# Layer 1's norm statistics from 16 products, with gate projections and VectorE/GpSimd work reordered in layer 0

## The chip, the cores and the metric

The kernel runs on one core of one Trainium2 chip. The core has a matrix engine (TensorE, PE in the profile, with its weight loads as PEld), VectorE (DVE), ScalarE (ACT), GpSimd (POOL) and SyncE (SP), whose queue issues the DMAs. The metric is the device time of one execution in microseconds (us), as a median over runs.

## The reference, cut to what matters

A two-layer trunk over x of 512 tokens x 1024 channels, in float32. Each layer computes `x + rmsnorm(mixer(rmsnorm(x)))`.

```python
# layer 0: 16 SSD heads in 4 groups, 16 forgetting-attention heads, one projection in and one out
proj = einsum('bsd,de->bse', rmsnorm(x), w_in)        # z_ssd, z_fox, x/B/C, dt, q, k, v, f
xbc = silu(causal_depthwise_conv(xbc, conv_w, conv_b))   # width 4
y = ssd_chunked(xs, dt, a, bm, cm) + xs * d_skip      # chunks of 128; decay matrices exp(segment sums)
y = group_rmsnorm(y * silu(z_ssd))
o = forgetting_attention(q, k, v, log_f) * silu(z_fox)
out = einsum('bse,ed->bsd', concatenate([y, o]), w_out)
# layer 1
val, glu_gate, z = split(einsum('bsd,de->bse', rmsnorm(x), w_in))
h = causal_depthwise_conv(val * sigmoid(glu_gate), conv_w, conv_b)   # 2048 channels, width 31
h = silu(layernorm(h, ln_g, ln_b)) * silu(z)          # mean and variance over the 2048 channels
out = einsum('bse,ed->bsd', h, w_out)
```

## The kernel before, in words

**Products in three parts.** Every float32 operand of a large product is split into a high part (`hlh`, `uh`, `w`: a cast on ACT) and a low part (`hll`, `ul`: source minus high part, on DVE or POOL); each product is then three products of PE in a reduced float32 (`mm3`, L109).

**Jobs.** The input projection of layer 0 is a list of 48 jobs, numbered from 0, each of 24 products of 512 columns (or 48 of 256) with 512 KB of weights. SP loads a job's weights into one of two raw buffers `wr` (`wload`); `wsplit` casts them on ACT to `w` (L155, L157) and subtracts the low part on the job's engine `j.eng` (L119). Without other word `j.eng` is DVE for even and POOL for odd jobs (`Job`). Before the change the jobs are: B, C and two x tiles of group 0; eight `z_ssd`; B, C, x, x of groups 1, 2 and 3; four gate projections `z_fox(0..3)`; then `v_proj`, `qk_proj` for the eight pairs of heads, with `z_fox(4..7)` two after pair 1 and two after pair 2. A job's last action evacuates its PSUM bank: a width-4 convolution on ACT and DVE for B, C and x (`cv`), an ACT copy for the gates (`zf`), splits for q, k and v. For layer 1 most low parts are computed ahead during layer 0 (`lo_ahead`: `pre` loaded, `prh` cast on ACT, subtracted on DVE, stored as `lo`), so that layer 1 only casts.

**Steps between the products.** PE's order is written by hand (`manual_schedule` for PE); the other engines' queues are filled in an order that a scheduler picks, in which the weight casts have priority. `Steps` deals out the SSD and attention work between chunks of the projection's products: each step has needs with delays, counted in estimated PE time (`now`), and the remaining steps are spread evenly over the remaining chunks. SSD, per group g: Silu of B, C, x (`silus`), low parts of B and C on POOL, tokens-major transposes (`xt`, `Bt`), `cb`, and for each of four heads `seg` (segment sums, four DVE instructions, then Exp on ACT), `mprod` (L1331: `seg` times `cb` on DVE, then cast to `hlh` on ACT and low part `hll` on POOL) and `ydiag` (12 products of 64 columns into `yd`), then states, gate and norm. Attention, per head: four `sa` (scores `s`, negated maximum on DVE, Exp `pr` on ACT, scaling on POOL), four `sb` (transposes `pT`, split `ph`, `pl`), one `sc` (`o`). `fox_silus(a)` is the Silu of four gates in place (`zf<-zf`); it runs once its four projections are there. Silu and Exp need different tables on ACT: a switch is an ACT_TABLE_LOAD.

**From layer 0 to layer 1.** After the output projection, `done0` norms each block of 128 tokens into `u`; `to_uT` (L362) transposes `u` on PE into `uT` banks, from which ACT makes `uh1` (L375, in PSUM reads of 256 tokens) and DVE `ul1` (L380). It is called for layer 0 at the very start, and for layer 1 twice, for the first and the second half of the tokens. The first four jobs of layer 1 (small weight tiles `ws`) run on the first half and then on the second. A weight cast looks at the list `evacs`: it is queued behind the last listed ACT instruction that was issued at least three jobs earlier (`cast`, L151). Only the Sigmoid and z evacuations of layer 1 entered themselves there (`evacuated`).

**Layer 1.** Sixteen tiles of 128 channels: value and gate products, GLU, then 31 convolution taps shared by DVE (`lane`), ACT with POOL (`pool_stream`, `prod` and `acc`) and, for the last two tiles, PE. `tile_end` squares the finished tile `cvo` on ACT to `sq`, and keeps running totals `Ssum` and `Qsum` on POOL, of the first 14 tiles. `stats1` then sums over channels: for each of four token blocks and both totals, three one-column products (total, tile 14, tile 15) into one bank `st`; DVE and POOL make mean and `rstd`, and `stats2` spreads them over partitions by products (`mu`, `rs`). Two z jobs stand on PE between `stats1` and `stats2`, one behind it; then the output projection starts with `lnorm` (DVE), Silu and split per tile.

Of the kernel before, what the change touches and what calls it, by code (L numbers as in the profile page):

```python
# [11 lines left out]
AF = mybir.ActivationFunctionType  # L12
ALU = mybir.AluOpType
# [5 lines left out]
NB = S // P  # L19
# [17 lines left out]
def trunk(  # L37
# [7 lines left out]
    V, G, A, T = nc.vector, nc.gpsimd, nc.scalar, nc.tensor  # L45
# [55 lines left out]
    def mm(o, l, r, start, stop):  # L101
        T.matmul(o, l, r, start=start, stop=stop, skip_group_check=True)  # L102
        now[0] += max(o.shape[-1] / 2400 + 0.014, 0.11)
# [10 lines left out]
    def tok(b):  # L114
        return slice(b * P, (b + 1) * P)
# [5 lines left out]
    def hilo(src, n=S, eng=None, s="hl", cast=None):  # L121
        h, l = t2(s + "h", F32R)[:, :n], t2(s + "l", F32R)[:, :n]
        split(h, l, src, cast or A.copy, eng or V)
        return h, l
# [23 lines left out]
    def evacuated(i):  # L148
        evacs.append((state["run"], i.ins))
# [71 lines left out]
    jobs = []  # L221
# [140 lines left out]
    def to_uT(uh, ul, half, us, g0):  # L362
        for kp in range(KT // 2):
            pb = bank("uT")
            for j in range(2):
                k = 2 * kp + j
                for b in range(2):
                    tr(pb[:, j * 256 + b * P : j * 256 + (b + 1) * P],
                                us[b][k // 4][:, k % 4 * P : (k % 4 + 1) * P], ident)
            for j in range(2):  # L370
                k = 2 * kp + j
                sl = slice(half * 256, half * 256 + 256)
                src = pb[:, j * 256 : (j + 1) * 256]
                g = g0[:, k : k + 1]
                A.activation(uh[k][:, sl], src, AF.Copy, scale=g)  # L375
            for j in range(2):
                k = 2 * kp + j
                src = pb[:, j * 256 : (j + 1) * 256]
                g = g0[:, k : k + 1]
                V.scalar_tensor_tensor(ul[k][:, sl], src, g, f32(uh[k])[:, sl], ALU.mult, ALU.subtract)  # L380
# [39 lines left out]
    pb = bank("pv")  # L420
# [89 lines left out]
    def xbc(kind, i):  # L510
        base, t0 = BASE[kind]

        def evac(pb):
            bcx[kind, i] = conv4(pb, t0 + i)
            done[kind, i] = now[0]
        return fm_job(e_w_in, base + i * P, evac, uh, ul)
# [51 lines left out]
    def z_fox(j):  # L568
        def evac(pb):
            oT[j] = t2("zf")  # L570
            A.copy(oT[j], pb)
            done["zf", j] = now[0]
        fm_job(e_w_in, C_ZF + j * P, evac, uh, ul)
# [130 lines left out]
    z_ssd(0)  # L704
    z_ssd(1)
    for g in range(1, 4):
        xbc("B", g)
        xbc("C", g)
        xbc("x", 2 * g)
        xbc("x", 2 * g + 1)  # L710
    for j in range(4):
        z_fox(j)
    for j in range(8):
        if j % 2 == 0:
            v_proj(j // 2)
        qk_proj(j)
        if j in (1, 2):
            for i in range(2):
                z_fox(2 + 2 * j + i)

    x1, us1 = [], []
    uh1, ul1 = {}, {}
# [247 lines left out]
    def tile_end(j, a):  # L970
        o = acc[j]
        if not NPT[j // 2]:
            A.copy(o, a)
        sq = t2("sq")
        A.activation(sq, o, AF.Square)
        sums.append((o, sq))
        if len(sums) == 2:
            n = [t2("Ssum"), t2("Qsum")]
            for i in range(2):
                G.tensor_tensor(n[i], sums[0][i], sums[1][i], ALU.add)  # L980
            tot.extend(n)
        elif 2 < len(sums) <= NT - 2:
            for i in range(2):
                G.tensor_tensor(tot[i], tot[i], sums[-1][i], ALU.add)

    tot = []
    lanes = [lane(0), lane(1)]
# [42 lines left out]
    def stats1():  # L1030

        pb = bank("st")
        parts = [tot, sums[-2], sums[-1]]
        for b in range(NB):
            for i in range(2):
                o = pb[:, 4 * i + b : 4 * i + b + 1]
                for n, t in enumerate(parts):
                    mm(o, t[i][:, tok(b)], ones[:, 0:1], n == 0, n == 2)
        mq = st["mq"] = col("mq", 8)
        V.tensor_scalar(mq, pb[:, :8], 1.0 / 2048, None, ALU.mult)  # L1040
        va = col("va", 4)
        V.tensor_tensor(va, mq[:, :4], mq[:, :4], ALU.mult)
        V.tensor_tensor(va, mq[:, 4:8], va, ALU.subtract)
        V.tensor_scalar(va, va, 0.0, EPS, ALU.max, ALU.add)
        rs = st["r"] = col("rstd4", 4)
        G.tensor_tensor(rs, va, mhalf.to_broadcast([P, 4]), ALU.pow)
        for i, c in enumerate((mq, rs)):
            dm = st["d", i] = t2("dm")
            for b in range(NB):
                V.tensor_scalar(dm[:, tok(b)], ident, c[:, b : b + 1], None, ALU.mult)  # L1050
# [278 lines left out]
    def mprod(h):  # L1329
        s = ms[h]  # L1330
        V.tensor_tensor(s, s, SG[h // 4]["cb"], ALU.mult)  # L1331
        ms[h] = hilo(s, eng=G)

    def ydiag(h):
        st = SG[h // 4]
# [82 lines left out]
    def attention(steps):  # L1418
# [50 lines left out]
        for h in range(16):  # L1469
# [14 lines left out]
                add(("sb", h, i), lambda h=h, i=i: sb(h, i), *need)  # L1484
            add(("sc", h), lambda h=h: sc(h), (("sb", h, 3), 6), (("v", h // 4), 5), (("fs", h // 8), 3))

    early = lo_ahead([j for j in jobs[J1:] if not j.make][:48])
    run(1)
    steps = Steps()
# [78 lines left out]
```

## Time and profile before

| what | value |
|---|---|
| median of 3 timed runs | 984.03 us (981.89 to 984.90) |
| the profiled execution: its time, its span | 978.23 us, 976.5 us |
| mean granted TensorE clock in it | 0.97 |
| PE, DVE, ACT, POOL busy, share of the span | 96%, 74%, 61%, 50% |
| layer 0 with its output projection | 0 to 605 us |
| layer 1's statistics products | 850.8 to 858.0 us |

The page gives busy time by engine, the granted clock of TensorE, the chain of work that ended last, and groups of instructions by line and operation. Timelines list instructions in order of time: start, duration, engine, line, operation, output <- inputs, count, and in brackets how long the engine stood idle before and for whom. Matmuls are pipelined: one row's duration is its latency, and what a product costs is the distance to the next start. A clock of 0.50 means that TensorE runs at half speed.

### The profile page before, as it was taken

The page shows a single profiled execution, that of the slowest core. Times are in us where ns is not written, and L with a number is a line of the kernel's source. Part 1 is how long each engine was busy: PE and PEld are TensorE (multiplying, and loading weights), DVE is VectorE, ACT ScalarE, POOL GpSimd, SP SyncE. Part 2 cuts the span into 40 slices and gives each one's busy share as a digit, 9 for nine tenths or more (in the row PEclk, how much of TensorE's full clock was granted, in tenths as well). Part 3 has the DMA queues.
Part 4 walks back from the last instruction along what each step waited for, and adds up shares of the span by engine and source line. Part 5 has one row for each costly group of instructions (what it writes and reads, how often), then busy time and mean ns, then how long its engine had stood idle before and what let it go on. Part 6 is the DMA issues. An engine that isn't in the chain of part 4 may idle for free.

```text
span 976.5 us, 13762 instructions
## 1 busy us (share of the span) xinstructions
PE 934.1 (96%) x4723; PEld 777.3 (80%) x4723; DVE 718.0 (74%) x1217; ACT 598.3 (61%) x1075; POOL 488.2 (50%) x424
## 2 busy tenths in 40 slices
PE   5999999989999989989999998999999999999996
PEld 5976887777988868878678888888888887787885
DVE  5767868978476758887866246999998989549812
ACT  5556666567456756757674446788696768437500
POOL 2313545243233413533562101999999998439610
PEclk9999999979699999999899998999999999989999
DMA  6636432364446576573527795254664753513422
GB/s 181 209 93 205 151 93 64 104 192 145 138 130 196 170 240 201 181 230 132 187 88 236 257 361 201 81 188 143 218 191 135 233 188 132 163 57 108 141 75 108
DMA packets 180266, 159.84 MB, mean 164 GB/s; under 512 B 7708, under 2 KB 151716, under 8 KB 180196
## 3 DMA queue, kind: packets, MB, share of 16 engines
q1 hardware_dynamic: 180180, 158.96, 50.7%
q8 instruction: 37, 0.61, 0.2%
q14 instruction: 33, 0.27, 0.1%
q10 hardware_dynamic: 16, 0.00, 0.0%
HBM read 129.45 MB, written 29.36 MB: 163 GB/s over the span
## 4 chain that ended last, share of the span: by engine, by line
PE 64%; DVE 11%; issue 7%; DMA 6%; ACT 6%; POOL 5%; SPq 1%; DVEq 0%; ACTq 0%; POOLq 0%
PE m L102 38%; PE o L102 10%; PE tm L102 6%; POOL w L119 3%; PE yd L102 3%; DMA wr<-in_o_w_in_dram 2%; DMA wr<-in_e_w_out_dram 2%; ACT w L157 2%; PE s L102 1%; DVE pre L205 1%; PE acc L102 1%; PE pT L106 1%; ACT pr L95 1%; PE st L102 1%; DVE nmx L1432 1%
## 5 line engine op out<-in xcount | busy, mean ns | idle before, releaser
L102 PE MATMUL m<-uh,w 128*128 128x512 f32 (+1 forms) x1392 | 457.6, 395 | 3.1 <-DVE cv L505 1.9
L102 PEld LDWEIGHTS m<-uh,w 128*128 128x128 f32 x1392 | 262.8, 191 | 55.1 <-issue 3.1
L102 PE MATMUL m<-ul,w 128*128 128x512 f32 (+1 forms) x696 | 268.9, 386 | 0.0
L119 POOL TENSOR_TENSOR w<-wr,w 128x1024 fp32r<-128x1024 f32 x44 | 112.0, 2545 | 164.7 <-ACT w L157 115.6
L961 DVE SCALAR_TENSOR_TENSOR acc<-h,cw,acc 128x490 f32<-128x490 f32 (+14 forms) x272 | 177.6, 728 | 5.2 <-ACT acc L953 4.5
L102 PE MATMUL o<-w,hlh 128*128 128x512 f32 x512 | 161.7, 397 | 2.0 <-ACT pr L95 1.9
L868 POOL TENSOR_TENSOR acc<-acc,prod 128x505 f32<-128x505 f32 (+12 forms) x122 | 156.6, 1285 | 7.4
L102 PEld LDWEIGHTS m<-ul,w 128*128 128x128 f32 x696 | 132.9, 191 | 21.1 <-issue 0.5
L157 ACT CAST w<-wr 128x1024 fp32r<-128x1024 f32 x76 | 79.6, 1049 | 54.2 <-DMA wr<-in_e_w_out_dram 17.3
L102 PEld LDWEIGHTS o<-w,hlh 128*128 128x128 f32 x512 | 94.9, 190 | 21.1 <-ACT pr L95 2.5
L102 PE MATMUL o<-w,hll 128*128 128x512 f32 x256 | 101.2, 395 | 1.8 <-DVE hll L119 1.6
L1438 POOL TENSOR_SCALAR pr<-pr,ri 128x128 f32<-128x128 f32 (+1 forms) x64 | 38.8, 608 | 117.3 <-DVE ri L1437 93.4
L205 DVE TENSOR_TENSOR pre<-pre,prh 128x1024 fp32r<-128x1024 f32 x48 | 71.3, 1486 | 34.5 <-ACT prh L204 34.2
L102 PE MATMUL tm<-w,uh 128*128 128x256 f32 (+1 forms) x384 | 94.8, 339 | 0.6 <-ACT pr L95 0.6
L119 DVE TENSOR_TENSOR w<-wr,w 128x1024 fp32r<-128x1024 f32 x44 | 59.4, 1350 | 35.1 <-ACT w L157 28.0
L854 ACT ACTIVATE prod<-h,cw 128x505 f32<-128x505 f32 (+12 forms) x122 | 77.5, 707 | 0.0
L155 ACT CAST w<-wr 128x1024 fp32r<-128x1024 f32 x56 | 57.6, 1047 | 31.0 <-DMA wr<-in_o_w_out_dram 13.3
L102 PEld LDWEIGHTS tm<-w,uh 128*128 128x128 f32 x384 | 66.1, 200 | 6.5 <-issue 1.1
L341 POOL TENSOR_TENSOR rstd<-var,mhalf 128x1 f32<-128x1 f32 (+1 forms) x20 | 12.9, 644 | 114.2 <-DVE var L339 114.1
L204 ACT CAST prh<-pre 128x1024 fp32r<-128x1024 f32 x48 | 50.5, 1052 | 21.6 <-DVE pre L205 14.0
L102 PE MATMUL tm<-w,ul 128*128 128x256 f32 (+1 forms) x192 | 63.2, 329 | 0.0
L95 ACT ACTIVATE pr<-s,nmx 128x128 f32<-128x128 f32 (+1 forms) x64 | 33.9, 530 | 46.5 <-DVE nmx L1432 32.4
(265 smaller groups left out, 1605.2 us busy)
## 6 DMA issues: line engine op xcount, KB each, us to landing
wr<-in_e_w_in_dram SPq DMA_DIRECT2D x56, 512.0 KB
pre<-in_o_w_in_dram SPq DMA_DIRECT2D x48, 512.0 KB
lo<-pre SPq DMA_DIRECT2D x48, 512.0 KB
wr<-in_o_w_in_dram SPq DMA_DIRECT2D x48, 512.0 KB
w<-lo SPq DMA_DIRECT2D x44, 512.0 KB
wr<-in_e_w_out_dram SPq DMA_DIRECT2D x16, 512.0 KB
wr<-in_o_w_out_dram SPq DMA_DIRECT2D x16, 512.0 KB
x<-in_x_dram SPq DMA_DIRECT2D x12, 256.0 KB
```

What stands on the lines that cost most here:

```text
L95: i = A.activation(*a, **kw)
L102: T.matmul(o, l, r, start=start, stop=stop, skip_group_check=True)
L119: lo_eng.tensor_tensor(lo, src, f32(hi), ALU.subtract)
L155: last_cast[0] = A.copy(hi, src).ins
L157: last_cast[0] = A.copy(hi, src).ins
L204: A.copy(h, t)
L205: V.tensor_tensor(t.bitcast(F32R), t, f32(h), ALU.subtract)
L341: mark["rstd"] = G.tensor_tensor(r, v, mhalf.to_broadcast([P, ss.shape[-1]]), ALU.pow).ins
L854: A.activation(prs[i][:, s:], hs[j][:, : S - s], AF.Copy, scale=w31(30 - s, j))
L868: G.tensor_tensor(a2[j][:, s:], a2[j][:, s:], prs.pop(i)[:, s:], ALU.add)
L961: V.scalar_tensor_tensor(a[:, s:], h[:, : S - s], w31(30 - s, j), a[:, s:], ALU.mult, ALU.add)
L1438: G.tensor_scalar(p[:, :L], p[:, :L], ri, 1.0, ALU.mult, ALU.mult)
```

## The change

Five edits:

- The totals take in tiles 14 and 15, these two adds on DVE, and `stats1` makes 16 products in place of 48.
- `to_uT` for layer 1 enters its ACT reads in `evacs`.
- `z_fox(4..7)` stands ahead of the B, C and x jobs of group 3.
- The low part in `mprod` goes from POOL to DVE.
- The jobs 6 to 39 all subtract on POOL.

```diff
--- before.py
+++ after.py
@@ -372,7 +372,9 @@
                 sl = slice(half * 256, half * 256 + 256)
                 src = pb[:, j * 256 : (j + 1) * 256]
                 g = g0[:, k : k + 1]
-                A.activation(uh[k][:, sl], src, AF.Copy, scale=g)
+                i = A.activation(uh[k][:, sl], src, AF.Copy, scale=g)
+                if state["run"]:
+                    evacuated(i)
             for j in range(2):
                 k = 2 * kp + j
                 src = pb[:, j * 256 : (j + 1) * 256]
@@ -704,6 +706,9 @@
     z_ssd(0)
     z_ssd(1)
     for g in range(1, 4):
+        if g == 3:
+            for j in range(4, 8):
+                z_fox(j)
         xbc("B", g)
         xbc("C", g)
         xbc("x", 2 * g)
@@ -714,9 +719,6 @@
         if j % 2 == 0:
             v_proj(j // 2)
         qk_proj(j)
-        if j in (1, 2):
-            for i in range(2):
-                z_fox(2 + 2 * j + i)
 
     x1, us1 = [], []
     uh1, ul1 = {}, {}
@@ -979,9 +981,9 @@
             for i in range(2):
                 G.tensor_tensor(n[i], sums[0][i], sums[1][i], ALU.add)
             tot.extend(n)
-        elif 2 < len(sums) <= NT - 2:
+        elif len(sums) > 2:
             for i in range(2):
-                G.tensor_tensor(tot[i], tot[i], sums[-1][i], ALU.add)
+                (G if len(sums) <= NT - 2 else V).tensor_tensor(tot[i], tot[i], sums[-1][i], ALU.add)
 
     tot = []
     lanes = [lane(0), lane(1)]
@@ -1030,12 +1032,9 @@
     def stats1():
 
         pb = bank("st")
-        parts = [tot, sums[-2], sums[-1]]
-        for b in range(NB):
-            for i in range(2):
-                o = pb[:, 4 * i + b : 4 * i + b + 1]
-                for n, t in enumerate(parts):
-                    mm(o, t[i][:, tok(b)], ones[:, 0:1], n == 0, n == 2)
+        for i in range(2):
+            for b in range(NB):
+                mm(pb[:, 4 * i + b : 4 * i + b + 1], tot[i][:, tok(b)], ones[:, 0:1], True, True)
         mq = st["mq"] = col("mq", 8)
         V.tensor_scalar(mq, pb[:, :8], 1.0 / 2048, None, ALU.mult)
         va = col("va", 4)
@@ -1329,7 +1328,7 @@
     def mprod(h):
         s = ms[h]
         V.tensor_tensor(s, s, SG[h // 4]["cb"], ALU.mult)
-        ms[h] = hilo(s, eng=G)
+        ms[h] = hilo(s)
 
     def ydiag(h):
         st = SG[h // 4]
@@ -1484,6 +1483,8 @@
                 add(("sb", h, i), lambda h=h, i=i: sb(h, i), *need)
             add(("sc", h), lambda h=h: sc(h), (("sb", h, 3), 6), (("v", h // 4), 5), (("fs", h // 8), 3))
 
+    for j in jobs[6:40]:
+        j.eng = G
     early = lo_ahead([j for j in jobs[J1:] if not j.make][:48])
     run(1)
     steps = Steps()
```

ACT's queue where layer 1's input is transposed (`uh` here is `uh1`, `junk` a sum of squares of the next token block, `wr` the raw weights). Before:

```order
L375 ACTIVATE uh_1333_6103<-uT_6119,c_130 128x256
L375 ACTIVATE uh_1335_6105<-uT_6119,c_130 128x256
L157 CAST w_6569<-wr_6567 128x1024
L375 ACTIVATE uh_1337_6107<-uT_6128,c_130 128x256
L375 ACTIVATE uh_1339_6109<-uT_6128,c_130 128x256
L375 ACTIVATE uh_1341_6111<-uT_6137,c_130 128x256
L375 ACTIVATE uh_1343_6113<-uT_6137,c_130 128x256
L157 CAST w_6574<-wr_6572 128x1024
L375 ACTIVATE uh_1345_6115<-uT_6146,c_130 128x256
L375 ACTIVATE uh_1347_6117<-uT_6146,c_130 128x256
L348 ACTIVATE junk_6165,ss_6164<-o_1252_5746 128x512
```

After the change:

```order
L375 ACTIVATE uh_1333_6103<-uT_6119,c_130 128x256
L375 ACTIVATE uh_1335_6105<-uT_6119,c_130 128x256
L375 ACTIVATE uh_1337_6107<-uT_6128,c_130 128x256
L375 ACTIVATE uh_1339_6109<-uT_6128,c_130 128x256
L375 ACTIVATE uh_1341_6111<-uT_6137,c_130 128x256
L375 ACTIVATE uh_1343_6113<-uT_6137,c_130 128x256
L375 ACTIVATE uh_1345_6115<-uT_6146,c_130 128x256
L375 ACTIVATE uh_1347_6117<-uT_6146,c_130 128x256
L348 ACTIVATE junk_6165,ss_6164<-o_1252_5746 128x512
L348 ACTIVATE junk_6183,s_1362_6182<-o_1244_5731 128x512
```

The two casts between the `uh` reads have gone; they, and the two casts that stood ahead of this piece, now come later, between the products of layer 1's first two tiles.

ACT's queue where the second four gates get their Silu. Before, inside attention (`pr` is the Exp of scores `s`):

```order
L95 ACTIVATE pr_3640,rs_3641<-s_3634,nmx_3638 128x128
L571 COPY zf_3646<-m_3537 128x512
L95 ACT_TABLE_LOAD
L95 ACTIVATE zf_2985<-zf_2985 128x512
L95 ACTIVATE zf_3067<-zf_3067 128x512
L95 ACTIVATE zf_3535<-zf_3535 128x512
L95 ACTIVATE zf_3646<-zf_3646 128x512
L95 ACT_TABLE_LOAD
L95 ACTIVATE pr_3677,rs_3678<-s_3671,nmx_3675 128x256
```

After the change these four stand in the SSD work of group 2, behind its `seg` Exps, and the Silus `cv` of group 3 follow under the same table:

```order
L95 ACTIVATE seg_1916<-seg_1916 128x512
L118 CAST hlh_1926<-seg_1869 128x512
L95 ACT_TABLE_LOAD
L95 ACTIVATE zf_1690<-zf_1690 128x512
L118 CAST hlh_1934<-seg_1880 128x512
L95 ACTIVATE zf_1780<-zf_1780 128x512
L1372 ACTIVATE yT_1943<-yT_1938,c_130 128x512
L1372 ACTIVATE yT_1953<-yT_1948,c_130 128x512
L118 CAST hlh_1959<-seg_1902 128x512
L95 ACTIVATE zf_1889<-zf_1889 128x512
L118 CAST hlh_1967<-seg_1916 128x512
```

The ACT_TABLE_LOAD in the second piece was there before, for the `cv` Silus; the two of the first piece are gone.

POOL's queue around the decay matrices of group 2 (`w`: low part of weights; `hll` from `cv`, `xe`, `seg`: low parts of B and C, of the decayed x, of the decay matrices). Before:

```order
L119 TENSOR_TENSOR w_1904<-wr_1795,w_1904 128x1024
L119 TENSOR_TENSOR hll_1645<-cv_1364,hlh_1644 128x512
L119 TENSOR_TENSOR hll_1649<-cv_1433,hlh_1648 128x512
L119 TENSOR_TENSOR w_2085<-wr_2010,w_2085 128x1024
L341 TENSOR_TENSOR rstd_1824<-var_1822,mhalf 128x4
L119 TENSOR_TENSOR hll_1841<-xe_1776,hlh_1840 128x512
L119 TENSOR_TENSOR hll_1867<-xe_1806,hlh_1866 128x512
L119 TENSOR_TENSOR w_2291<-wr_2178,w_2291 128x1024
L119 TENSOR_TENSOR hll_1936<-seg_1875,hlh_1935 128x512
L119 TENSOR_TENSOR hll_1944<-seg_1886,hlh_1943 128x512
L119 TENSOR_TENSOR hll_1969<-seg_1911,hlh_1968 128x512
L119 TENSOR_TENSOR hll_1977<-seg_1925,hlh_1976 128x512
```

After the change:

```order
L119 TENSOR_TENSOR w_1696<-wr_1621,w_1696 128x1024
L119 TENSOR_TENSOR w_1786<-wr_1699,w_1786 128x1024
L119 TENSOR_TENSOR w_1895<-wr_1789,w_1895 128x1024
L119 TENSOR_TENSOR hll_1645<-cv_1364,hlh_1644 128x512
L119 TENSOR_TENSOR hll_1649<-cv_1433,hlh_1648 128x512
L119 TENSOR_TENSOR w_1995<-wr_1898,w_1995 128x1024
L119 TENSOR_TENSOR w_2068<-wr_1998,w_2068 128x1024
L341 TENSOR_TENSOR rstd_1818<-var_1816,mhalf 128x4
L119 TENSOR_TENSOR hll_1835<-xe_1773,hlh_1834 128x512
L119 TENSOR_TENSOR hll_1861<-xe_1800,hlh_1860 128x512
L119 TENSOR_TENSOR w_2148<-wr_2071,w_2148 128x1024
L119 TENSOR_TENSOR w_2207<-wr_2151,w_2207 128x1024
```

Every job's `w` is now POOL's, and the four `hll<-seg` have left for DVE, where each stands behind the products `seg<-seg,cbs`.

## Prediction

> **What bounds the kernel now.** I read the page first, then the clock and the busy times by stretch, then TensorE's (PE's) waits, and last the timelines of the places that the diff touches. The page's head and its chain:
>
> ```profile
> span 976.5 us, 13762 instructions
> ...
> PE 934.1 (96%) x4723; PEld 777.3 (80%) x4723; DVE 718.0 (74%) x1217; ACT 598.3 (61%) x1075; POOL 488.2 (50%) x424
> ...
> PE 64%; DVE 11%; issue 7%; DMA 6%; ACT 6%; POOL 5%; SPq 1%; DVEq 0%; ACTq 0%; POOLq 0%
> ```
>
> PE is the bound, so a change pays only where it takes products from PE, ends a wait of PE, or keeps PE's clock up. The stretches that matter (busy us, with counts, of PE, PEld, DVE, ACT, POOL; then the granted clock, DMA share, GB/s):
>
> ```profile
> 0.00:605.00 605.00, 572.75 (x3100) 481.51 (x3100) 424.23 (x733) 367.73 (x685) 218.19 (x209) 0.96 0.56 177
> 650.00:800.00 150.00, 150.00 (x663) 124.22 (x662) 141.62 (x225) 114.44 (x183) 143.11 (x114) 1.00 0.59 188
> 350.00:500.00 150.00, 139.55 (x794) 114.72 (x793) 115.75 (x217) 99.32 (x212) 63.40 (x77) 0.97 0.58 189
> 102.90:116.50 13.60, 13.60 (x90) 12.25 (x89) 13.13 (x17) 8.14 (x12) 8.58 (x4) 1.00 0.65 195
> 205.30:215.50 10.20, 10.20 (x38) 9.04 (x38) 8.97 (x10) 7.14 (x11) 5.04 (x4) 0.50 0.74 233
> 246.30:263.30 17.00, 17.00 (x81) 17.00 (x81) 7.02 (x9) 6.23 (x10) 3.17 (x3) 0.50 0.58 180
> 365.70:369.10 3.40, 3.40 (x10) 2.55 (x10) 2.66 (x6) 2.61 (x6) 2.48 (x2) 0.50 0.00 0
> 587.60:594.40 6.80, 5.72 (x25) 5.42 (x26) 3.95 (x10) 4.18 (x10) 0.55 (x1) 0.50 1.02 343
> 853.80:860.70 6.90, 6.90 (x28) 6.32 (x28) 2.08 (x12) 0.00 (x0) 1.02 (x1) 0.51 0.19 70
> ```
>
> Layer 1's middle (650 to 800) is PE without a gap at full clock: nothing to win there. Layer 0 (up to 605) leaves PE idle for 32 us, and in five of these rows the clock stands at half.
>
> **The change part by part.** *The statistics of layer 1.* The chain in order of time (start, us, what), then PE's, DVE's and ACT's timelines around them:
>
> ```profile
> 839.92 10.88 PE m L102 x48
> 850.80 7.16 PE st L102 x48
> 857.96 12.36 PE m L102 x48
> ```
> ```profile
> 850.64 0.28 PE L102 MATMUL st<-ones,Ssum 128*128 128x1 f32 x2
> 853.23 0.36 PE L102 MATMUL st<-ones,Ssum 128*128 128x1 f32 x2
> ```
> ```profile
> 845.38 0.69 DVE L966 TENSOR_TENSOR cvo<-acc,acc 128x512 f32<-128x512 f32 x1 [2.61 <-POOL acc L876]
> 846.11 0.63 ACT L975 ACTIVATE sq<-cvo 128x512 f32<-128x512 f32 x1 [0.76 <-DVE cvo L966]
> ```
>
> The 24 one-column products from 850.64 to 853.23 take 0.108 us each; the other 24 stand mostly at half clock. Sixteen take 16 x 0.108 = 1.7 us, not 7.16: -5.4. The half clock of 853.8 to 860.7 also slows the wide products from 857.96 to 860.7, which lose half of 2.7 us. It sets in after 3 us of nothing but one-column products. At 102.9 to 116.5, where batches of 12 narrow `yd` products alternate with wide ones, the clock stayed at 1.00, and 1.7 us of narrow ones between wide ones is like that; so I take the halving away as well: -1.4. Together **-6.8**. The two new pairs of adds wait on DVE: the last for `sq`, which ends at 846.74. An add has the form of the 0.69 us row, so the sums are done by 847.5, and PE needs them at 850.64: 3 us of cover. Queued behind them on DVE is only `mq`, which waits for these products anyway. All that follows (48 wide products, the `mu` products, the output projection) is a PE chain with fixed cover, so the 6.8 arrive at the end.
>
> The Trainium skill (TensorE: Matmul & The Clock Gate, Part 1) says that the clock falls after an idle window of about 3.4 us. By that rule the halving at 853.8 could not come from these products, since PE was busy for all 6.90 us of the row, and would stay, now over wide products alone (2 us more lost there): the term would be about -3.4. The row differs from the rule, and I go by the row.
>
> *Layer 1's transposed input.* `to_uT` now enters its ACT reads in `evacs`, so the weight casts of the jobs from the fifth of layer 1 on are queued behind them. Now (ACT, then PE, then the chain):
>
> ```profile
> 581.37 0.84 ACT L375 ACTIVATE uh<-uT,c 128x256 fp32r<-128x256 f32 x2 [0.78 <-PE uT L106]
> 586.90 1.04 ACT L157 CAST w<-wr 128x1024 fp32r<-128x1024 f32 x1 [4.70 <-DMA wr<-in_o_w_in_dram]
> 590.48 0.83 ACT L375 ACTIVATE uh<-uT,c 128x256 fp32r<-128x256 f32 x2
> 591.20 0.60 ACT L348 ACTIVATE junk<-o 128x512 f32<-128x512 f32 x1
> ```
> ```profile
> 588.38 0.58 PE L102 MATMUL m<-uh,ws 128*128 128x256 f32 x1 [3.02 <-ACT uh L375]
> 603.31 1.86 PE L106 MATMUL uT<-ident,u 128*128 128x128 f32 x15 [0.71 <-DVE u L360]
> ```
> ```profile
> 562.92 7.39 DMA wr<-in_o_w_in_dram
> ```
>
> A cast stood in ACT's queue for 4.70 us until its weights landed, with six `uh` reads behind it; PE waited 3.02 us for them and then ran its next 6 us (588.4 to 594.4) at half clock, 3 lost. That is -6.0 on PE. The other path gives the same: the rows of the second half start with `junk` at 591.20, right behind the eighth `uh`. Eight reads at 0.42 from 581.37 end at 584.8, 6.4 earlier, and this chain ends in the `u` for which PE waited at 603.31. I take **-6.3**. Ends: -7 if the rest of the waits goes too; 0 if it is paid back by the four casts that now come late. They stand among the products for tiles 0 and 1, and the third must wait for a load that starts only when the first frees its buffer: up to 7.39 us, with POOL's products behind it. PE has two jobs in hand by then (2 x 24 products at 10.88/48 = 0.227, so 10.9 us), and DVE's spare in 650 to 800 is 8.4 us: covered, hence nothing.
>
> *The gate projections moved ahead of group 3.* Now the second Silu batch of the attention gates stands between two table loads inside attention (ACT, then PE):
>
> ```profile
> 359.42 1.28 ACT L95 ACT_TABLE_LOAD   x1
> 360.72 2.19 ACT L95 ACTIVATE zf<-zf 128x512 f32<-128x512 f32 x4
> 362.92 1.28 ACT L95 ACT_TABLE_LOAD   x1
> ```
> ```profile
> 364.84 0.50 PE L102 MATMUL s<-KS,QS 128*128 128x512 f32 x1 [3.75 <-ACT pr L95]
> ```
>
> PE waits 3.75 us for it and then runs 3.4 us at half clock (365.7:369.1). In the new order these four activations follow a Silu table that group 2 loads anyway; two loads are gone, and so are 3.75 + 1.7 = **-5.5**. What is late next is attention itself: its first two pairs of q and k, with their DMAs from `chl` on SP, come four jobs (4 x 24 x 0.227 = 21.8 us) later, and its steps crowd into fewer jobs. The weight loads go through SP in the new order in the same number. Lower end 0 (PE's order is the same again before attention ends); upper end 10.5, as much PE idleness again as the row 350:500 has (150 - 139.55). Between them I take **+4**, nearer the lower end, because DVE, the busiest helper there, has 34 of 150 us free.
>
> *POOL and DVE change places in layer 0.* Seventeen weight subtractions (the even jobs from 6 to 39) go from DVE to POOL; the sixteen low parts of the decay matrices (`hll` from `seg`) go from POOL to DVE. PE's wait, the groups (count | busy us, mean ns | idle before), and single rows:
>
> ```profile
> PE yd L102 <- POOL hll L119: 3.0, 2, 2.0
> ```
> ```profile
> L119 POOL TENSOR_TENSOR w<-wr,w 128x1024 fp32r<-128x1024 f32 x44 | 112.0, 2545 | 164.7 <-ACT w L157 115.6
> L119 DVE TENSOR_TENSOR w<-wr,w 128x1024 fp32r<-128x1024 f32 x44 | 59.4, 1350 | 35.1 <-ACT w L157 28.0
> L119 POOL TENSOR_TENSOR hll<-seg,hlh 128x512 fp32r<-128x512 f32 x16 | 24.9, 1570 | 19.3 <-ACT hlh L118 19.3
> ```
> ```profile
> 178.12 0.68 DVE L119 TENSOR_TENSOR hll<-xt,hlh 128x512 fp32r<-128x512 f32 x1
> 179.92 2.92 DVE L119 TENSOR_TENSOR w<-wr,w 128x1024 fp32r<-128x1024 f32 x1
> 235.47 1.21 DVE L119 TENSOR_TENSOR w<-wr,w 128x1024 fp32r<-128x1024 f32 x1
> 179.37 2.39 POOL L119 TENSOR_TENSOR w<-wr,w 128x1024 fp32r<-128x1024 f32 x1 [7.42 <-ACT w L157]
> ```
>
> POOL gets 17 x 2.545 - 24.9 = +18.4 us, DVE 17 x 1.35 - 16 x 0.68 = 12.1 us less. POOL has the room (218 of 605). The two waits of `yd` for POOL (3.0 us) stand just before the half clock rows of 205.3 and 246.3, which cost 10.2/2 + 17.0/2 = 13.6. If a decay part comes from DVE in 0.68 rather than 1.57 us, and not behind a weight subtraction, both waits and both halvings can go: -16.6. Against it, the new DVE instruction waits for ACT's `hlh` cast, and the state updates `H` and the next subtractions of `pre` stand behind it; and a DVE subtraction that starts while POOL's runs is held: 2.92 us at 179.92 against 1.21 alone, that is, 1.84 us until POOL's ends at 181.76 and then its own time. If all of POOL's added 18.4 us held DVE, it would have 18.4 - 12.1 = 6.3 us more. Ends +6.3 and -16.6; I take half the gain, **-8.3**, since the removed waits are sure to shrink but whether the clock then stays up depends on a few tenths.
>
> The Trainium skill (SBUF: State Buffer, "SBUF: two separate sides") gives that hold as a rule: a POOL instruction and a DVE one with two SBUF inputs lock each other out of a shared port pair for a whole instruction. The two rows at 179 agree to 0.1 us. It speaks against this edit, and by it alone the term would be the +6.3.
>
> Sum: -6.8 - 6.3 - 5.5 + 4 - 8.3 = -22.9. The profiled execution took 978.23 us (span 976.5), 5.8 under the median 984.03 of the three timed ones; I set the difference against the median: **961**.
>
> **The rivals.** (1) *Group 2 and 3 lose all their waits and halvings* and attention loses nothing: -6.8 - 6.3 - 5.5 - 16.6 = -35.2, 949. For it: the full-clock row of 102.9, where the same narrow products run without a wait. Against it: ACT's casts pace `yd` too. (2) *POOL's longer queue holds DVE* and DVE becomes the bound of the SSD groups: -18.6 + 6.3 + 4 = -8.3, 976. For it: the 2.92 us row. Against it: DVE's work there falls. It is the Trainium skill's port rule above, carried to its end. (3) *Late weights in layer 1*: the boundary's 6.3 is paid back: 967. Against it: the cover worked out above. (4) *Both ends at once*, the held DVE and the crowded attention: -18.6 + 6.3 + 10.5 = -1.8, 982, no change. (5) *Slower: attention is paced by its own loop* (scores, DVE maximum, ACT Exp, POOL scaling, transposes), not by PE's queue, so its start, 21.8 us later, moves the end of layer 0 by as much: -18.6 + 21.8 = +3.2, 987. It decides from 18.6 us of unrecovered delay. For it: PE's idle 10.5 us in 350:500 are waits on that loop. Against it: PE is busy for 93% of that stretch, so most of the delay is other work done earlier. That the edits do not do what they say is out for the products and the table loads, which the program's rows fix.
>
> **How the numbers follow.** Forecast 0.52; rivals 0.16, 0.14, 0.06, 0.05 and 0.07. A measurement of this kernel can tell about 0.3% (3 us) from no change. Faster: 0.52 + 0.16 + 0.14 + 0.06 = 0.88; same 0.05; slower 0.07. The range takes in the first three rivals with a microsecond beyond their figures: 948 to 977; the last two, 0.12, stay out.
>
> **What would show it.** 16 `st` products in under 2 us with the clock at 1.00 behind them; `uh` reads in one run without a cast, and no halving near 590; no table load inside attention; `yd` not waiting for POOL, and the clock at full in groups 2 and 3; DVE rows of 2.9 us no more frequent. I am wrong if PE's idle time in attention grows by more than 10 us, if PE waits for `w` from POOL, or if the halvings only move elsewhere.

## The result, and the profile after

The changed kernel takes 957.12 us (median of 4 runs, 954.05 to 962.36) against 984.46 us for the kernel before in the same comparison (981.89 to 989.71): the ratio is 0.9721, with a 95% interval from 0.9656 to 0.9786. The forecast was 961 us, 948 to 977, and faster. The profiled execution took 954.4 us (span 952.5), 24.0 us less than the span of before. The head of the page and its chain:

```profile
span 952.5 us, 13693 instructions
...
PE 911.9 (96%) x4691; PEld 757.7 (80%) x4691; DVE 736.3 (77%) x1220; ACT 594.5 (62%) x1073; POOL 503.3 (53%) x425
...
PE 69%; DVE 11%; issue 6%; ACT 5%; POOL 4%; DMA 3%; SPq 1%; DVEq 0%; POOLq 0%; ACTq 0%
```

PE is the bound as before. DVE, which the prediction wanted 12.1 us lighter, is 18.3 us heavier (718.0 before). By stretch (columns as in the prediction: busy us of PE, PEld, DVE, ACT, POOL, then the granted clock, DMA share, GB/s):

```profile
0.00:590.00 590.00, 561.24 (x3128) 471.83 (x3129) 442.09 (x743) 364.49 (x690) 235.96 (x211) 0.99 0.56 178
88.70:92.10 3.40, 3.40 (x9) 1.93 (x8) 3.40 (x5) 1.19 (x3) 2.15 (x2) 0.50 0.87 251
232.05:235.45 3.40, 2.83 (x10) 2.26 (x10) 3.23 (x5) 1.17 (x2) 0.00 (x0) 0.50 0.92 261
409.50:416.30 6.80, 5.74 (x28) 5.16 (x26) 5.59 (x14) 3.47 (x9) 4.48 (x5) 0.50 0.91 284
467.60:471.00 3.40, 3.40 (x12) 2.27 (x10) 2.29 (x8) 1.91 (x7) 2.58 (x5) 0.50 0.07 20
831.40:844.20 12.80, 12.80 (x66) 10.84 (x65) 3.54 (x13) 3.07 (x4) 1.02 (x1) 1.00 0.39 134
```

Layer 0 still leaves PE idle for about 29 us (590 - 561.24; it was 32). What fell is the half clock. Besides the five rows that the prediction quotes, before has two more at half clock:

```profile
85.80:89.20 3.40, 3.40 (x10) 2.12 (x8) 3.40 (x4) 1.17 (x3) 2.53 (x2) 0.50 0.85 261
478.40:485.20 6.80, 6.08 (x20) 4.57 (x19) 5.16 (x14) 4.26 (x12) 2.98 (x6) 0.50 0.23 66
```

Without the end of the last products, where both kernels drop to half, the seven of before sum to 54.5 us (44.3 and 10.2), the four of after to 17. The statistics, 831.4 to 844.2, run at full clock.

Where the 24.0 us came from is read from the first and last starts of a few products. The scores `s` of attention, the transposes `uT` and the products `mu` behind the statistics, first of before and then of after:

```profile
L102 PE MATMUL s<-KS,QS x64: 218/333/498, 287.1 to 501.6; 128*128 128x128 f32 x16, 128*128 128x256 f32 x16, 128*128 128x384 f32 x16, 128*128 128x512 f32 x16
L106 PE MATMUL uT<-ident,u x32: 270/272/331, 580.7 to 604.9; 128*128 128x128 f32 x32
L102 PE MATMUL mu<-dm,ones x8: 272/275/275, 870.1 to 870.9; 128*128 128x128 f32 x8
```
```profile
L102 PE MATMUL s<-KS,QS x64: 218/333/522, 300.7 to 489.2; 128*128 128x128 f32 x16, 128*128 128x256 f32 x16, 128*128 128x384 f32 x16, 128*128 128x512 f32 x16
L106 PE MATMUL uT<-ident,u x32: 270/272/331, 568.3 to 585.7; 128*128 128x128 f32 x32
L102 PE MATMUL mu<-dm,ones x8: 272/275/275, 844.2 to 845.0; 128*128 128x128 f32 x8
```

Up to the last `s` 12.4 us are gained; up to the first `uT` it is still 12.4. From there to the first `uT` of the second half (602.33 before, 583.59 now) come 6.3 more. The statistics start at 831.48 against 850.64, 19.2 earlier, and `mu` 25.9 earlier: 6.8 there. Behind `mu`, where the two kernels run the same products, 1.9 are given back. The next two views are PE's chain over the statistics, and ACT and PE at the boundary, all of after:

```profile
831.64 1.68 PE st L102 x16
833.32 11.06 PE m L102 x48
844.37 0.91 PE mu L102 x8
```
```profile
568.96 3.03 ACT L375 ACTIVATE uh<-uT,c 128x256 fp32r<-128x256 f32 x8 [3.75 <-issue]
571.83 0.65 ACT L348 ACTIVATE junk<-o 128x512 f32<-128x512 f32 x1
584.15 1.86 PE L106 MATMUL uT<-ident,u 128*128 128x128 f32 x15 [0.29 <-DVE u L360]
```

Both are as forecast: `st` takes 1.68 us, the eight `uh` reads stand together with no cast among them, and `junk` follows at once. Layer 0 is another matter: the same 12.4 us could come from either of its two edits, or from one against the other. Four kernels with one edit each (the two of the exchange count as one) were run to separate them.

### The profile page after: what moved, and what is told of

It is laid out like the page before. It is cut to its first block, busy times and chain, and to the rows that moved or that the text cites. A ratio compares the mean times of both kernels' runs of the same rounds, so it can differ in the third digit from the quotient of the medians.

```text
span 952.5 us, 13693 instructions
## 1 busy us (share of the span) xinstructions
PE 911.9 (96%) x4691; PEld 757.7 (80%) x4691; DVE 736.3 (77%) x1220; ACT 594.5 (62%) x1073; POOL 503.3 (53%) x425
## 4 chain that ended last, share of the span: by engine, by line
PE 69%; DVE 11%; issue 6%; ACT 5%; POOL 4%; DMA 3%; SPq 1%; DVEq 0%; POOLq 0%; ACTq 0%
PE m L102 39%; PE o L102 17%; PE tm L102 5%; POOL w L119 3%; DMA wr<-in_e_w_in_dram 2%; PE s L102 2%; DVE pre L205 2%; ACT w L157 2%; DVE hll L119 2%; PE pT L106 1%; PE yd L102 1%; PE acc L102 1%; DVE w L119 1%; DVE cvo L1062 1%; DVE cvo L1061 1%
## 5 line engine op out<-in xcount | busy, mean ns | idle before, releaser
L102 PE MATMUL m<-uh,w 128*128 128x512 f32 (+1 forms) x1392 | 452.7, 392 | 1.8 <-POOL w L119 1.8
L119 POOL TENSOR_TENSOR w<-wr,w 128x1024 fp32r<-128x1024 f32 x61 | 150.3, 2467 | 188.5 <-ACT w L157 151.0
L205 DVE TENSOR_TENSOR pre<-pre,prh 128x1024 fp32r<-128x1024 f32 x48 | 75.0, 1563 | 38.6 <-ACT prh L204 26.9
L1437 POOL TENSOR_SCALAR pr<-pr,ri 128x128 f32<-128x128 f32 (+1 forms) x64 | 41.7, 653 | 104.4 <-DVE ri L1436 84.3
L102 PEld LDWEIGHTS o<-w,hll 128*128 128x128 f32 x256 | 48.4, 189 | 17.2 <-DVE hll L119 7.3
L95 ACT ACTIVATE pr<-s,nmx 128x128 f32<-128x128 f32 (+1 forms) x64 | 33.8, 529 | 36.3 <-DVE nmx L1431 22.9
```

Source lines behind the costliest of these rows:

```text
L95: i = A.activation(*a, **kw)
L119: lo_eng.tensor_tensor(lo, src, f32(hi), ALU.subtract)
L205: V.tensor_tensor(t.bitcast(F32R), t, f32(h), ALU.subtract)
L1437: G.tensor_scalar(p[:, :L], p[:, :L], ri, 1.0, ALU.mult, ALU.mult)
```

## The experiments

Ratios are against the kernel before, from five rounds with both on the same chip, with a 95% interval; us are worked out from the ratio and the median of before in that comparison (979 to 981). The timings of before in these comparisons scatter by about 1%.

**1. The statistics alone.** The edits of `tile_end` and `stats1` as in the diff, nothing else.

> The kernel before with the statistics edit alone (16 one-column products from totals over all 16 tiles). My theory (the half clock behind the statistics comes from their one-column products): `st` takes under 2 us, the clock stays at full behind it, and the time falls by 6.8 us, to about 0.993 of before. Rival (the half clock comes from elsewhere and stays): -3.4 us, 0.9965, with a halved stretch still near the `m` products that follow. Rival (the two pairs of adds on DVE are late): PE waits for them and the gain is under 3 us.

Measured 0.9883 (0.9836 to 0.9931), -11.5 us. Its chain:

```profile
847.67 1.68 PE st L102 x16
849.35 11.06 PE m L102 x48
860.40 0.91 PE mu L102 x8
```

From the first `st` to the first `mu` it takes 12.7 us, 19.5 before: the 6.8 of the forecast to a tenth. No half clock is left there, so the case in which it would have stayed (-3.4) falls; its 0.9965 lies outside the interval as well. PE has no wait for the adds on DVE. The timed gain is larger than 6.8, which stands at the interval's end. In this profiled execution layer 0, whose instructions are the same in the same order, ran with less half clock than in that of before, and the first `st` comes 3.1 us earlier (the last section); whether the rest of the timed gain is such scatter, no run decides.

**2. The transposed input alone.** `evacuated(i)` behind ACT's read in `to_uT`, nothing else.

> The kernel before with only the ACT reads of layer 1's transposed input entered ahead of the weight casts. My theory: the second half's transposes come 6.3 us earlier, no halving near 590, and the 6.3 us reach the end: 0.9936. Rival (the casts that now come late starve PE in layer 1's first tiles): the gain is paid back and the ratio is 1.000, with PE waits for `w` between 600 and 650.

Measured 0.992 (0.9889 to 0.9951), -7.8 us. All PE waits of this kernel from 596 to 680 us (waiter, releaser: us, times, longest):

```profile
PE m L102 <- DVE ul L382: 0.3, 1, 0.3
PE uT L106 <- DVE u L360: 0.3, 1, 0.3
```

No wait for `w`: the later casts cost nothing, as the cover of 10.9 us had it. The transposes stretch over 17.4 us instead of 24.2.

**3. The gate projections alone.** Moved as in the diff, nothing else.

> The kernel before with only the last four gate projections moved ahead of group 3. My theory of the prediction: two table loads go and with them 5.5 us, attention starts about 22 us later and loses 4: -1.5 us, 0.9985 (-5.5 to +5). Rival (attention is paced by its own loop): +3 or more, over 1.003. Rival (the later, denser attention leaves PE fewer idle slots and group 3 gains the product time as cover for its waits): -8 or more, under 0.992.

Measured 0.9774 (0.9712 to 0.9836), -22.1 us: nearly the whole change. The stretch from 183 to 264 us (groups 2 and 3) of before, the same of this kernel, and this kernel's `s`:

```profile
183.00:264.00 81.00, 76.10 (x382) 64.93 (x382) 57.75 (x103) 48.19 (x77) 29.15 (x19) 0.83 0.55 169
```
```profile
183.00:264.00 81.00, 81.00 (x457) 67.91 (x455) 68.94 (x108) 60.43 (x92) 35.32 (x20) 1.00 0.71 224
```
```profile
L102 PE MATMUL s<-KS,QS x64: 218/334/523, 289.4 to 476.9; 128*128 128x128 f32 x16, 128*128 128x256 f32 x16, 128*128 128x384 f32 x16, 128*128 128x512 f32 x16
```

PE has neither idle time nor half clock there, although the engines of the decay matrices are those of before and `hll` still comes from POOL. `yd` no longer waits for it. The last case on record, cover for group 3, is the one that came, with more than twice its 8 us. Attention starts 2.3 us later than before, with four jobs (21.8 us of products) more behind it: 21.8 - 2.3 = 19.5 us gained in the groups. From the first to the last `s` it takes 187.5 us, against 214.5 - 21.8 = 192.7: 5.2 gained in attention.

**4. The exchange between POOL and DVE alone.** `hilo(s)` in `mprod` and `jobs[6:40]` on POOL, nothing else.

> The kernel before with only POOL and DVE changed round in layer 0: decay matrices' low parts on DVE, the subtractions of jobs 6 to 39 on POOL. My theory: `yd` no longer waits for POOL in groups 2 and 3, half of 16.6 us gained: -8.3, 0.9915. Rival (POOL's longer queue holds DVE and PE): +6.3, 1.006, with PE waits for `w` or `hll` from POOL in groups 0 and 1. Rival (all waits and halvings of groups 2 and 3 go): -16.6, 0.983.

Measured 1.0007 (0.9967 to 1.0047): no change, neither the -8.3 nor the +6.3. In its trace the wait of `yd` at 243.5 and the 17.0 us of half clock behind it are gone, but the start of group 1, its first `cb`, comes 5.5 us later. Before, then this kernel:

```profile
144.82 0.22 PE L102 MATMUL cb<-hlh,hlh 128*128 128x128 f32 x1
```
```profile
150.30 0.22 PE L102 MATMUL cb<-hlh,hlh 128*128 128x128 f32 x1
```

The four measured gains sum to 11.5 + 7.8 + 22.1 - 0.7 = 40.7 us, and the change has 27.3 (984.46 - 957.12). The intervals of the five are wide, so this is a hint only that something in the change takes from the rest; the next experiment tests it.

**5. The change without the exchange.**

```diff
-        ms[h] = hilo(s)
+        ms[h] = hilo(s, eng=G)
...
-    for j in jobs[6:40]:
-        j.eng = G
```

> The kernel after with the exchange between POOL and DVE undone (low parts of the decay matrices on POOL, the weights' subtractions as before); statistics, boundary and moved gate projections stay. Theory from the four edits alone (-10.0, -6.4, -23.0 and 0): the three add, -36 to -39 us against before, ratio 0.96, and the kernel after is beaten by 10 us or more because the exchange lengthens the first two groups by 5 us and has no waits left to remove in groups 2 and 3. Rival (the edits overlap, and the exchange is neutral here as it is alone): the same time as the kernel after, 0.972.

Measured 0.9631 (0.9584 to 0.9677), 942.8 us: the first theory. It beats the changed kernel by 0.0090 of before, with half-intervals of 0.0047 and 0.0065 that combine to 0.0080: 1 to 17 us; and the spans differ by 14.5 (938.0 and 952.5). With that of experiment 6, which its interval doesn't tell from it, it is the fastest kernel of this study. Its page; its `s`; then a group of each kernel that differs, DVE's scaling of `y` up to 300 us (count | busy us, mean ns), without the exchange and in after; and the low parts on DVE in after:

```profile
PE 908.9 (97%) x4691; PEld 755.9 (81%) x4691; DVE 722.3 (77%) x1221; ACT 594.5 (63%) x1073; POOL 493.8 (53%) x424
```
```profile
L102 PE MATMUL s<-KS,QS x64: 218/333/522, 291.1 to 477.7; 128*128 128x128 f32 x16, 128*128 128x256 f32 x16, 128*128 128x384 f32 x16, 128*128 128x512 f32 x16
```
```profile
L1362 DVE TENSOR_SCALAR y<-y,rstd 128x256 f32<-128x256 f32 x16 | 7.8, 532 | 4.5 <-POOL rstd L341 4.5
```
```profile
L1362 DVE TENSOR_SCALAR y<-y,rstd 128x256 f32<-128x256 f32 x16 | 11.6, 775 | 4.5 <-POOL rstd L341 4.5
L119 DVE TENSOR_TENSOR hll<-seg,hlh 128x512 fp32r<-128x512 f32 x16 | 16.6, 1039 | 1.8 <-ACT hlh L118 1.8
```

The exchange should have taken 12.1 us from DVE and gives it 14.0 (736.3 - 722.3). The low parts take 1039 ns on average, not 680, and other DVE work grows with them. How PE comes to wait for it is seen at two places of after: DVE's and POOL's timeline, then PE's, then PE's waits of the whole kernel:

```profile
113.67 2.85 DVE L119 TENSOR_TENSOR hll<-seg,hlh 128x512 fp32r<-128x512 f32 x1
113.30 2.67 POOL L119 TENSOR_TENSOR w<-wr,w 128x1024 fp32r<-128x1024 f32 x1 [0.64 <-ACT w L157]
228.85 2.97 DVE L1362 TENSOR_SCALAR y<-y,rstd 128x256 f32<-128x256 f32 x3 [1.12 <-POOL rstd L341]
228.98 2.43 POOL L119 TENSOR_TENSOR w<-wr,w 128x1024 fp32r<-128x1024 f32 x1 [0.16 <-ACT w L157]
```
```profile
231.62 0.62 PE L106 MATMUL yT<-ident,y 128*128 128x128 f32 x2 [1.96 <-DVE y L1362]
```
```profile
PE yT L106 <- DVE y L1362: 3.5, 3, 2.0
PE cb L102 <- POOL hll L119: 3.5, 1, 3.5
PE yo L102 <- DVE hll L119: 2.3, 1, 2.3
```

A low part that takes 0.68 us alone takes 2.85 while POOL subtracts (POOL's ends at 115.97, DVE's at 116.52; 115.97 + 0.68 is 116.65), and `yo` waits for what is queued behind it on DVE. Three scalings, 0.34 us each where the next one stands alone (232.40), take 2.97 beside POOL's 2.43; PE waits 1.96 for them, and the half clock sets in at 232.05. In the kernel without the exchange the waits of `yT` and `yo` are not there, and that of `cb` is 1.9. These are the rows that speak for the Trainium skill's rule (SBUF — State Buffer, "SBUF: two separate sides"), that a DVE instruction with two SBUF inputs and a POOL one lock each other out of a port pair for a whole instruction; `y` has one SBUF input only, and the page counts a DVE instruction in a two-port mode as well. In which mode `y` runs, no row here shows.

**6 and 7. Which half of the exchange.** The changed kernel with `jobs[6:40]` back on their engines; and the changed kernel with the low parts back on POOL.

> The kernel after with only the subtractions of jobs 6 to 39 given back to their engines of before; the low parts of the decay matrices stay on DVE. Theory (POOL's longer queue is what costs): as fast as the kernel after without any exchange, 0.96, the first two groups 5 us shorter than after. Rival (DVE's added 16 low parts delay its weights): no better than after, 0.972.

Measured 0.9655 (0.9608 to 0.9702), 943.2 us, first `cb` of group 1 at 144.1 (149.8 in after). By the ratios alone it isn't told from after (0.0066 apart, 0.0080 is the combined half-interval). The traces tell them apart: the last `s` stands at 477.5 here and at 477.7 in experiment 5, and at 487.2 to 497.0 in the four executions with the subtractions on POOL (after, experiments 7, 11 and 12). So the subtractions on POOL are what costs, and the low parts on DVE cost nothing that shows without them.

> The kernel after with only the low parts of the decay matrices given back to POOL, which keeps the subtractions of jobs 6 to 39. Theory (POOL's queue is what costs, and the low parts are then queued in it too): slower than after by 5 us or more, 0.98, with PE waiting for `hll` from POOL. Rival (DVE freed of the low parts gains more): faster than after by 5, 0.967.

Measured 0.9717 (0.9675 to 0.9758), 951.2 us: by the ratios the same as after, within 8 us either way. The theory's "slower by 5" found no support: the span is 5.1 us shorter than that of after (947.4). With the subtractions on POOL, who makes the low parts makes no difference that these runs can tell.

**8 and 9. Why the moved gate projections gain.** In the first kernel the last four stand right behind the first four, after group 3; in the second the first four stand ahead of group 3 and the last four stay in attention.

```diff
-    for j in range(4):
+    for j in range(8):
         z_fox(j)
...
-        if j in (1, 2):
-            for i in range(2):
-                z_fox(2 + 2 * j + i)
```

> The kernel before with the last four gate projections right behind the first four, after group 3, not ahead of it. Theory A (the move gains because their products stand ahead of group 3 and give its and group 2's helpers time): no gain in groups 2 and 3, half clocks near 205 and 246 as in before; only the table loads and the wait for them go, -5.5 us, 0.994. Theory B (the move gains by what it takes out of attention): -20 us or more, 0.978, with half clocks near 205 and 246 still there.

Measured 0.9985 (0.9957 to 1.0013), -1.5 us. Theory A has the groups right, half clock and waits as in before, but its -5.5 us for the table loads did not come (0.994 lies outside). The rows of groups 2 and 3 and PE's wait:

```profile
183.00:264.00 81.00, 72.90 (x357) 58.97 (x357) 60.66 (x108) 50.16 (x81) 30.21 (x19) 0.89 0.54 166
```
```profile
PE yd L102 <- POOL hll L119: 2.3, 1, 2.3
```

```diff
+        if g == 3:
+            for j in range(4):
+                z_fox(j)
...
-    for j in range(4):
-        z_fox(j)
```

> The kernel before with the first four gate projections ahead of group 3; the other four stay among the attention's q and k, with their table loads and the wait for them. Theory (four jobs with one ACT copy behind each, in the place of four that put conv work on DVE, give groups 2 and 3 the time to prepare `yd`): no wait of `yd` for POOL and no half clock near 205 and 246; about what the moved last four gained less the 1.5 to 5.5 us of the table loads: -15 to -20 us, 0.98 to 0.985. Rival (only the last four gain, by leaving attention): no gain, 1.000, with q and k as early as before.

Measured 0.9837 (0.9791 to 0.9883), -16.0 us, as expected. Groups 2 and 3, and `s`:

```profile
183.00:264.00 81.00, 81.00 (x468) 68.73 (x469) 70.33 (x119) 54.61 (x88) 32.54 (x25) 1.00 0.67 208
```
```profile
L102 PE MATMUL s<-KS,QS x64: 218/333/503, 267.6 to 485.3; 128*128 128x128 f32 x16, 128*128 128x256 f32 x16, 128*128 128x384 f32 x16, 128*128 128x512 f32 x16
```

Attention has as much behind it as before and starts 19.5 us earlier, the same 19.5 as in experiment 3; then it takes 217.7 us, 3.2 more than before. So the place ahead of group 3 makes the gain, whichever four projections stand there. What they do there is seen in two groups of before: a job of B, C or x leaves three convolution steps on DVE (48 in all), a gate projection one copy on ACT:

```profile
L505 DVE SCALAR_TENSOR_TENSOR cv<-m,c,cv 128x511 f32<-128x511 f32 (+2 forms) x48 | 34.9, 742 | 10.2 <-ACT cv L503 9.7
```
```profile
L571 ACT COPY zf<-m x8: 571/578/590, 216.9 to 358.8; 128x512 f32<-128x512 f32 x8
```

With 21.8 us more of products between the same helper work, POOL's and DVE's parts of `yd` are ready in time, and PE fills the time in which it waited and ran at half clock. Whether four jobs with convolution steps behind them would have covered as well was not tried.

**10. Two ahead of group 3, two in attention**, on the kernel of experiment 5.

> The kernel after without the exchange, and with only two gate projections (the fifth and sixth) ahead of group 3; the last two stand among the attention's q and k. Theory (the cover of group 3 is what gains, and two jobs give half of it): one of the two half clocks or `yd` waits of groups 2 and 3 is back; 0.97, 7 us slower than with four. Rival (attention, which idles PE for 20 us between 350 and 475, gains by having two jobs more): faster than with four, 0.958.

Measured 0.9684 (0.9634 to 0.9734), 945.8 us: one half clock (6.8 us at 203.7) and one wait of `yd` (1.6 us) are back, as the theory had it, but what it lacks to experiment 5 (5 us by the ratios) is within the intervals. Attention did not gain from having more jobs: from the first to the last `s` it takes 197.8 us, against 186.6 + 10.9 = 197.5 in experiment 5 with the products of two more. The 20 us of idle PE named beforehand are not there either: in experiment 5's kernel PE is idle for 6 us between 350 and 475.

**11 and 12. What halves the clock at the statistics.** The changed kernel with its statistics' products run three times over (48 in a row), once plain and once with products of 256 columns among them whose result is not used. One run each.

> The kernel after with each of the 16 statistics products run three times, 48 one-column products in a row as in before, but from the totals. Theory (one-column products alone halve the clock): a halved stretch starts during or right behind them, and from the first `st` to the first `mu` it takes 19 us, as in before, against 12.7 in after. Rival (the half clock of before came from a wait or from the kind of its operands): full clock, 12.7 + 32 x 0.108 = 16.2 us.

```profile
831.10:833.20 2.10, 2.10 (x21) 2.10 (x19) 0.00 (x0) 1.53 (x2) 0.00 (x0) 1.00 1.05 372
833.20:843.40 10.20, 10.20 (x40) 9.33 (x40) 2.21 (x12) 0.00 (x0) 1.02 (x1) 0.50 0.20 68
```

From the first `st` to the first `mu` it takes 21.1 us (19 expected, 16.2 by the rival), 8.4 more than in after, of which the 32 more products at 0.108 are 3.5. The rest is the half clock, which begins 2.1 us after the first of them, with PE busy all along. So one-column products alone bring it. The other runs bear it out: in all seven executions of this study with 48 in a row the clock halves there, 2.1 to 4.9 us after the first, and in all six with 16 it does not.

> As the run with 48 one-column products, but with a product of 256 columns behind each of them (its result is not used). Theory (the clock goes by how much of the time PE streams columns): no half clock, 48 x (0.108 + 0.114) = 10.7 us for the block and 21.8 from the first `st` to the first `mu`. Rival (the length of the block or the one-column products themselves halve the clock): a halved stretch as without the wide products, 25 us or more.

```profile
839.30:845.10 5.80, 5.80 (x52) 5.78 (x51) 0.00 (x0) 1.53 (x2) 0.00 (x0) 1.00 0.70 246
845.10:851.90 6.80, 6.80 (x28) 6.32 (x28) 1.26 (x9) 0.00 (x0) 1.02 (x1) 0.50 0.00 0
```

The expectation was wrong about its own kernel: each one-column sum is two products in the trace, so a wide product stands behind every second one, 24 in all, and fills about a third of the time (half of the 0.227 of a product of 512 columns, in the 0.34 us from one pair to the next). The half clock came later (5.8 us after the first) and lasted 6.8 instead of 10.2, but it came, and from the first `st` to the first `mu` it took 22.3 us. So a third of wide work did not prevent the fall in this one run; whether it delays it, and what share would prevent it, is open, and the rival is not excluded.

## Why the prediction was right

The time was right (957 for 961, and -24.0 by trace for -22.9), in part by luck: of its five terms the first two were right, the next two about right in their sum, the fifth had the wrong sign, and a term that was missing made up for it. Point by point:

- *Statistics, -6.8*: measured -6.8 (experiment 1). The adds on DVE are covered (in after the last ends at 828.47, and the first `st` stands at 831.48), and the half clock goes with the products (experiment 11 brings it back).
- *Boundary, -6.3*: measured -6.3 in after, and 7.8 (4.8 to 10.9) alone. The casts that come late starve nobody (experiment 2). Rival 3 falls.
- *Table loads, -5.5, and attention, +4*: in sum -1.5, and what the four jobs bring without their place ahead of group 3 is -1.5 (experiment 8, -4.2 to +1.3). Attention took 188.5 us in after against 192.7 without the four jobs, 4.2 gained: it did not pay the +4, and rival 5, attention paced by its own loop, falls. PE's wait of 3.75 us went and its idle time in attention fell from 10.5 to 7.2 us. The 1.7 for the half clock did not come: attention has 10.2 us of it in both kernels, at 365.7 and 478.4 before and at 409.5 and 467.6 now.
- *The moved jobs as cover for groups 2 and 3*: this term was missing. "PE's order is the same again before attention ends" and "-5.5" looked only at the place that the jobs left. The place where they went gained 19.5 us (experiments 3 and 9).
- *Exchange, -8.3*: wrong in sign. The price of its upper end, +6.3 if all of POOL's added time holds DVE, was the right mechanism and too small: DVE is 14.0 us busier, and the last `s` comes 11.5 later than without the exchange (489.2 and 477.7). "The removed waits are sure to shrink" failed since the gate projections remove the same waits; alone, the exchange gains about what it costs (experiment 4).

For layer 0 the sum was -8.3 - 1.5 = -9.8, and -12.4 came out: -23.9 from the gate projections and the rest (501.6 to 477.7), +11.5 from the exchange. These are differences of single executions: the last `s` of three with before's layer 0 comes at 499.0 to 506.0, of three with after's at 488.8 to 497.0, so each figure carries several us of scatter, and the signs stand. Rivals 1 and 2 were set as alternatives and most of both took place: the waits of `yd` in groups 2 and 3 went, and the half clocks but for 3.4 us, by another edit than the one credited, and POOL's longer queue held DVE, on top, though PE stayed the bound. The five signs named beforehand read so in after. Three came (16 products in 1.68 us at full clock, `uh` in one run, no table load in attention). The fourth came in half: `yd` waits for nothing, but the clock falls once between the starts of groups 2 and 3, for 3.4 us at 232.05, behind the wait for the held scalings. The fifth, DVE rows held beside POOL no more frequent, did not come; that was the one to follow. Of the signs of being wrong, the halvings that only move were seen in attention.

## What to carry to other kernels

When jobs are moved in a list, price the place where they go as well as the one they leave: ahead of a stage whose helpers were late, four jobs with light follow-up work gained 19.5 us here (by the traces), and an exchange between the helpers nothing. Two edits that remove the same wait don't add up, and the one with a running cost is then all cost; so try each edit alone, and the whole without each. Work given to POOL to relieve DVE is priced by DVE's busy time after the change, not by what was taken off its queue.

## What the runs showed of the hardware

- The clock halves without any idle time of PE when its products are one column wide: with 48 in a row it fell 2.1 us after the first (experiment 11, 1.00 to 0.50 with PE busy for all 10.20 us), and with 16, in 1.68 us, it stayed at 1.00 (after). The Trainium skill (TensorE: Matmul & The Clock Gate, Part 1) speaks of an idle window; the row differs.
- How long the half clock lasts is not fixed by the code. At about 87 us after had 3.4 us of it and experiment 12, whose instructions are the same in the same order up to layer 1, had 20.5; from the first `tk`, a transpose at 66.0 and 66.6 us, to the first `cb` of group 1 it took 91.4 us there, 83.8 in after. In the stretch near 250, before had 17.0 and experiment 1, the same code there, 6.8:

```profile
87.30:107.80 20.50, 19.93 (x48) 13.45 (x49) 13.34 (x28) 8.52 (x13) 3.03 (x3) 0.50 0.53 176
```
```profile
250.00:256.80 6.80, 6.80 (x35) 6.80 (x34) 5.70 (x7) 5.03 (x8) 2.37 (x2) 0.50 0.37 120
```

  This is the size of the scatter between timings of one kernel, so a gain in one execution's layer 0 of under 10 us says little unless the rows show what made it.
